# Routing in program order on TensorE, six whole dense columns, and one chain for the last norms

## The chip, the cores and the metric

One core of one Trainium2 chip (trn2). The metric is the device time of one execution of the kernel in microseconds (us), as the median of the runs. Engines: TensorE (PE), VectorE (DVE), ScalarE (ACT), GpSimd (POOL), SyncE (SP), which here only issues DMAs.

## The reference

One decoder layer on 512 tokens of 1024 numbers (four tiles of 128 tokens, 0 to 3): attention and a state-space part first, then an expert stage (PEER), then a last norm. The change touches the expert stage and the last norm:

```python
def peer_ffn(x, w_q, sub1, sub2, u_tab, v_tab):          # x: normed tokens
    q = (xb @ w_q).reshape(b, 128, 8, 256)                # 8 heads
    s1 = einsum('bchd,kd->bchk', q[..., :128], sub1)      # scores against 128 subkeys
    s2 = einsum('bchd,kd->bchk', q[..., 128:], sub2)
    v1, i1 = top_k(s1, 16);  v2, i2 = top_k(s2, 16)
    top, sel = top_k(v1[..., :, None] + v2[..., None, :], 16)   # of 256 sums
    eidx = (i1 * 128 + i2)[sel]                           # 16 of 16384 experts, per head
    gate = softmax(top)
    hid = einsum('bcd,bchkd->bchk', xb, u_tab[eidx])
    act = gelu(hid) * gate
    return einsum('bchk,bchkd->bcd', act, v_tab[eidx])

h = h + peer_ffn(rms_norm(h, ffn_norm), ...)
return rms_norm(h, final_norm)                            # h * rsqrt(mean(h*h) + 1e-6) * g
```

## The kernel before

All instructions of four engines are recorded by a wrapper at line 134 (`Ordered`), so nearly every row of the trace has L134; rows are told apart by their operands. A tile scheduler orders each engine's instructions by its own model of costs, except where `with ordered(...)` is open: there the named engines keep the order in which the code issues them. Each engine then runs its instructions strictly in that order.

The expert stage has two forms. Tiles 0 and 1 are *sparse*: for each of 128 (head, k) pairs an expert step (`peer()`, `Steps`) gathers the u and v rows of that expert for 128 tokens by an indirect DMA from POOL (1.05 MB into one of five slots, `X` and `X4` in the trace), DVE makes the dot of u with the tokens (`CUSTOM_DVE_ANT_0`, its sum read out by a second instruction into `hid`), ACT makes the gelu, and v times the activation is added to h. For tile 0's last 20 steps (k from 108) this last part is done on PE: ACT scales the identity by the activation (`dg`), two fp32 matmuls of 128x512 add into two banks, and `flush()` adds the banks to h on DVE after step 127. The slot of a step is free for a new gather when its matmuls are done. Then `final(0, ...)` norms tile 0 and stores it.

Tiles 2 and 3 are *dense*: every one of 16384 experts is computed for their 256 tokens. For this `route([Topk(2), Topk(3)], ..., 256)` finds the gates of both tiles. It goes through 4 units of 2 heads. A unit has two banks of two times 8 fp32 matmuls 128x256 (q), an ACT copy of each bank, four matmuls with `c_subT` per tile (scores, into one bank per tile), and on DVE four scans of each bank (`first`) and the second top-k (`heads`). When all units are done `finish` transposes a tile's indices and gates on PE with `c_ident` (three 128x128 each) into a table `dtab`. The loop around it (`for w in rest()`) issues tile 0's last expert steps between the pieces of the routing.

Between the routing and the dense loop DVE works on 32 groups of `gate_tokens` (one 128x1024 and three 128x512 f16 products each), which turn `dtab` into the gates of the first 64 columns. The gates of the other 64 are made inside the loop, in its columns up to 61.

`dense()` loops over 128 columns j of 128 experts. Of each, a U half and a V half of 512 KB are loaded by SP (`load`, three buffers `raw`). ACT copies a half to fp32r (`hi`), DVE subtracts that from the raw one (`lo`), which frees the buffer and loads the next. PE then computes hid in 24 fp32r matmuls 128x256 (hi x hi, hi x lo, lo x hi), ACT the gelu (`gS`), DVE the product with the gates, ACT and DVE split that too (`acthi`, `actlo`), and `outp` adds 12 fp32r matmuls 128x512 into four banks. Each column also carries one sparse step of tile 1: a dot, two small ACT steps and an add on DVE. The loop runs with DVE, ACT, PE and POOL in program order. In it, tile 1's `final` is issued in the column of its last step.

After the loop the four banks are added to h of tiles 2 and 3 (held in HBM meanwhile), and `final` is run for each: a square with sum on ACT (`rms`), a chain of small DVE steps for the reciprocal square root (tiles `f_s`, `f_r`, `f_ri`), a scaling by it and the norm's weights, and one store of 512 KB.

Of the kernel before, what the change touches and what calls it, by code (L numbers as in the profile page):

```python
# [12 lines left out]
F32 = mybir.dt.float32  # L13
# [3 lines left out]
I32 = mybir.dt.int32  # L17
U32 = mybir.dt.uint32
AF = mybir.ActivationFunctionType
ALU = mybir.AluOpType  # L20
# [3 lines left out]
D = 1024  # L24
SEQ = 512
NT = 4
EPS = 1e-6
# [4 lines left out]
JC = 64  # L32
DENSE = (2, 3)
# [124 lines left out]
def paced(w, g):  # L158
    for _ in g:
        yield w  # L160
# [3 lines left out]
def hymba_kernel(ctx: ExitStack, tc: tile.TileContext, a, out, dbg=None):  # L164
    nc = tc.nc
    pins = set()
    V, S, G, PE = (Ordered(tc, e, n, pins) for e, n in ((nc.vector, "V"), (nc.scalar, "S"), (nc.gpsimd, "G"), (nc.tensor, "PE")))
    SP = nc.sync

    @contextmanager  # L170
    def ordered(*names):
        pins.update(names)
        yield
        pins.difference_update(names)
# [46 lines left out]
    def ct(name, shape, dt=F32):  # L221
        return cst.tile(list(shape), dt, name=name)


    def rsqrt(dst, src, tmp, itmp):
        V.tensor_scalar(itmp, src.bitcast(I32), -0.5, 1597463007.0, op0=ALU.mult, op1=ALU.add)
        y = itmp.bitcast(F32)
        for _ in range(3):
            V.tensor_tensor(tmp, y, y, op=ALU.mult)
            V.tensor_tensor(tmp, tmp, src, op=ALU.mult)  # L230
            V.tensor_scalar(tmp, tmp, -0.5, 1.5, op0=ALU.mult, op1=ALU.add)
            V.tensor_tensor(dst, tmp, y, op=ALU.mult)
            y = dst

    def rms(src, junk, n="n"):

        s2 = tiny.tile([128, 1], F32, name=n + "_s2")
        r2 = tiny.tile([128, 1], F32, name=n + "_r2")
        r1 = tiny.tile([128, 1], F32, name=n + "_r1")
        ri = tiny.tile([128, 1], I32, name=n + "_ri")  # L240
        S.activation(junk, src, AF.Square, accum_out=s2)
        V.tensor_scalar(s2, s2, 1.0 / D, EPS, op0=ALU.mult, op1=ALU.add)
        rsqrt(r2, s2, r1, ri)
        return r2
# [68 lines left out]
    dtab = msl.v([128, 4, 256], F16, off=4480)  # L313
# [9 lines left out]
    junk = ct("junk", [128, D], BF)  # L323
# [761 lines left out]
    def final(T, h, junk):  # L1085
        r2 = rms(h, junk, "f")
        V.scalar_tensor_tensor(h, h, r2, fn, op0=ALU.mult, op1=ALU.mult)
        SP.dma_start(out[T * 128:(T + 1) * 128, :], h)
# [146 lines left out]
    def dense(xh, xl, sp):  # L1235


        NE, n, done = 128, 128 - sp.k, 0
        acc = [bank() for _ in range(4)]
        his, los = [], []  # L1240
        raws = [lp.tile([128, 2048], F32, name=f"raw{i}") for i in range(2)] + [l01[0].v([128, 2 * D])]
        for i in range(2):
            his.append(lp.tile([128, 2048], F32R, name=f"hi{i}"))
            los.append(lp.tile([128, 2048], F32R, name=f"lo{i}"))
        acts = [lp.tile([128, 2, 256], F32R, name=f"act{i}") for i in range(2)]
        gS = [msl.v([128, 256], off=2048 + 1024 * i) for i in range(2)]
        half = (slice(0, D), slice(D, 2 * D))
        ring = [collections.deque(r[:, o] for r in raws) for o in half]
        loaded, hb = [{}, {}], {}

        def load(n):
            if ring[n] and nload[n] < NE:
                raw, j = ring[n].popleft(), nload[n]
                nload[n] += 1
                SP.dma_start(raw, a["uvt"][j][:, half[n]])  # L1255
                loaded[n][j] = raw

        def hi(j, n):
            if j < NE:
                S.activation(his[j % 2][:, half[n]], loaded[n][j], AF.Copy)  # L1260

        def lo(j, n):
            if j < NE:
                o = half[n]
                V.tensor_tensor(los[j % 2][:, o], loaded[n][j], his[j % 2].bitcast(F32)[:, o], op=ALU.subtract)
                ring[n].append(loaded[n].pop(j))
                load(n)

        def hid(j):
            if j < NE:  # L1270
                uh, ul = his[j % 2], los[j % 2]
                hb[j] = bank()
                for k in range(8):
                    ks = slice(128 * k, 128 * k + 128)
                    for i, (l, r) in enumerate(((uh, xh), (uh, xl), (ul, xh))):
                        PE.matmul(hb[j][:, 0:256], l[:, ks], r[:, k], start=(k == 0 and i == 0), stop=(k == 7 and i == 2))

        def gelu(j):
            if j < NE:
                b = hb.pop(j)  # L1280
                S.activation(gS[j % 2], b[:, 0:256], AF.Gelu_apprx_tanh)
                bfree(b)

        def gated(j):
            if j < NE:
                g = gS[j % 2].rearrange("p (q t) -> p q t", t=32)
                V.tensor_tensor(g, g, gates_of(j), op=ALU.mult)

        def acthi(j):
            if j < NE:  # L1290
                S.activation(acts[j % 2][:, 0], gS[j % 2], AF.Copy)

        def actlo(j):
            if j < NE:
                act = acts[j % 2]
                V.tensor_tensor(act[:, 1], gS[j % 2], act.bitcast(F32)[:, 0], op=ALU.subtract)

        def outp(j):
            (ah, al), vh, vl = (acts[j % 2][:, i] for i in range(2)), his[j % 2][:, D:], los[j % 2][:, D:]
            for t in range(2):  # L1300
                ts = slice(128 * t, 128 * t + 128)
                for i, (l, r) in enumerate(((ah, vh), (ah, vl), (al, vh))):
                    for n in range(2):
                        PE.matmul(acc[2 * t + n], l[:, ts], r[:, 512 * n:512 * n + 512], start=(j == 0 and i == 0),
                                  stop=(j == NE - 1 and i == 2), skip_group_check=True)

        def gate_group(j):

            for g in range(32):
                if 8 * (g // 4) - 1 + 2 * (g % 4) == j:  # L1310
                    return gate_parts(1, 8 * g, junk.bitcast(F32)[:, 0:256])
            return iter(())

        nload = [0, 0]
        for i in range(3):
            load(0)
            load(1)
        ngp = gate_group(-1)
        for i in range(2):
            hi(0, i)  # L1320
            lo(0, i)
        hid(0)
        gelu(0)
        hi(1, 0)
        lo(1, 0)
        for t0 in range(0, 256, 8):
            gate_tokens(0, t0)
        M.small = collections.deque(s for s in M.small if s.parent is nl)
        with ordered("V", "S", "PE", "G"):
            gated(0)  # L1330
            acthi(0)
            actlo(0)
            next(ngp)
            for j in range(NE):
                gp, ngp = ngp, gate_group(j)
                step = sp.k < 128 and (j + 1) * n > done * SPREAD
                hi(j + 2, 0)
                hi(j + 1, 1)
                next(gp, None)
                next(ngp, None)  # L1340
                if step:
                    sp.dot()
                hid(j + 1)
                if step:
                    sp.gelu()
                lo(j + 2, 0)
                gelu(j + 1)
                next(gp, None)
                gated(j + 1)
                next(gp, None)  # L1350
                acthi(j + 1)
                if step:
                    sp.add()
                    done += 1
                actlo(j + 1)
                outp(j)
                lo(j + 1, 1)
                if sp.k == 128 and step:
                    final(sp.T, xs[sp.T], junk)
                if j == 100:  # L1360
                    for i in range(2):
                        SP.dma_start(row(7)[:, half[i]], hsave[i])
        assert sp.k == 128
        for i, T in enumerate(DENSE):
            xs[T] = row(7)[:, half[i]]
            for n in range(2):
                V.tensor_tensor(xs[T][:, 512 * n:512 * n + 512], acc[2 * i + n], xs[T][:, 512 * n:512 * n + 512], op=ALU.add)
            final(T, xs[T], raws[i][:, 0:D])


    proj_k(0, w_k[1], G)
# [24 lines left out]
    for x in SEQN:  # L1396
# [12 lines left out]
        elif x == "F":  # L1409
# [3 lines left out]
            xs = [half(l01[0], 1)]  # L1413
# [12 lines left out]
    g2, fn = half(nl, 0), half(nl, 1)  # L1426
# [51 lines left out]
    W = dict(glu=0.75, k=3.45, c=2, q=3, cmp=3.45, att=0.45, mix=1.725, r1=1, route=0.65, gates=0.4)  # L1478
    NR = 2

    def rest():
# [48 lines left out]
        rl = []  # L1530
# [11 lines left out]
        yield from paced(W["r1"], both(route([Topk(1)], lambda k: X1[k // 4][:, k % 4], 128), later(), NR))  # L1542
        M.free(rl[0], *x1)
        state["p1"] = True
        yield from paced(W["route"], route([Topk(2), Topk(3)], lambda k: rl[1].v([128, 8, 256])[:, k], 256))
        M.free(rl[1])
        G.iota(io2, pattern=[[1, 128], [0, 2]], base=0, channel_multiplier=0, allow_small_or_imprecise_dtypes=True)
        M.group()
# [122 lines left out]
```

## Time and profile before

| | us |
|---|---|
| median of 3 runs | 1604.41 |
| lowest and highest run | 1602.51, 1612.80 |
| the profiled execution | 1603.72 |
| its span in the trace | 1602.0 |
| busy over the span: PE, DVE, ACT, POOL | 1374.4, 1460.7, 838.6, 524.4 |

The order of the stages in the span: attention and the state-space part with the sparse steps of tile 0 beside them up to about 640 us; the routing of tiles 2 and 3 with tile 0's last steps, to 772; gates and the first splits, to 833; the dense loop to about 1587; the last norms. In the rows, a timeline line is: start in us, duration in us, engine, line, operation, out<-in, count, and in brackets the idle time before it with what ended that. A line of the table by stretch is: from:to, length, busy time (and count) of PE, PE's weight loads, DVE, ACT and POOL, then the granted TensorE clock (1.00 is full speed), the share of DMA engines busy and GB/s. Records of fp32 matmuls come in pairs: one matmul is two records.

### The profile page before, as it was taken

The numbers are of one execution on the slowest core, as the hardware profiler recorded it, in microseconds if no ns is written. First come the engines' busy times: TensorE is split into PE (matmuls) and PEld (weight loads), VectorE is DVE, ScalarE is ACT, GpSimd is POOL, SyncE is SP. The second block draws the span as 40 slices with busy tenths as digits, with TensorE's granted clock in tenths as the row PEclk, the third lists the DMA queues.
The fourth block names the chain that finished last, engine by engine and source line by source line (L and its number), as shares of the span: only waits on it lengthen the run. The fifth ranks groups of instructions, "written<-read, shape, count | busy, mean of one in ns | idle before, by whom it ended". The sixth has DMA issues, their size and how long they took to land.

```text
span 1602.0 us, 24306 instructions
## 1 busy us (share of the span) xinstructions
PE 1374.4 (86%) x8400; PEld 1094.4 (68%) x8400; DVE 1460.7 (91%) x3324; ACT 838.6 (52%) x2078; POOL 524.4 (33%) x383
## 2 busy tenths in 40 slices
PE   5688794689868687897679999999999999999996
PEld 2366472456355355772468888888888999999995
DVE  8986179969899989799999999999999999999998
ACT  2345423646366654326565555555555555556563
POOL 6532012744352442012003333333333333333331
PEclk9897897788879799898659999999999999999998
DMA  6331478878898889318508999999999999999994
GB/s 265 106 106 66 172 285 298 337 315 337 325 373 333 315 340 419 131 52 342 211 3 327 334 344 337 343 332 340 341 340 363 388 374 382 374 375 375 378 375 168
DMA packets 88969, 469.48 MB, mean 293 GB/s; under 512 B 10253, under 2 KB 10893, under 8 KB 50701
## 3 DMA queue, kind: packets, MB, share of 16 engines
q0 software_dynamic: 37152, 268.98, 42.9%
q1 hardware_dynamic: 51692, 198.94, 34.4%
q8 instruction: 66, 1.08, 0.3%
q14 instruction: 59, 0.48, 0.1%
HBM read 464.74 MB, written 3.15 MB: 292 GB/s over the span
## 4 chain that ended last, share of the span: by engine, by line
DVE 25%; PE 22%; issue 4%; ACT 1%; DMA 1%; SPq 0%
PE bank L134 22%; DVE X L134 11%; DVE lo L134 8%; DVE junk L134 3%; DVE act L134 2%; DMA raw<-in_uvt 1%; ACT X L134 0%; DVE f_r L134 0%; DVE hid L134 0%; ACT hi L134 0%; ACT junk L134 0%; ACT raw L134 0%; DVE more L134 0%; ACT act L134 0%; SPq L1255 0%
## 5 line engine op out<-in xcount | busy, mean ns | idle before, releaser
L134 POOL DMA_INDIRECT X<-in_uv,eidx x256 | 430.7, 1682 | 955.2 <-DVE X L134 830.5
L134 ACT ACTIVATE X<-bank 128x256 f32<-128x256 f32 (+5 forms) x431 | 218.0, 520 | 181.7 <-PE bank L134 130.6
L134 PE MATMUL bank<-X 128*128 128x64 f16 (+10 forms) x1800 | 243.2, 285 | 71.0 <-DVE X L134 50.0
L134 PE MATMUL bank<-hi,act 128*128 128x512 f32 x1024 | 299.7, 394 | 0.0
L134 PE MATMUL bank<-XH,hi 128*128 128x256 f32 x1024 | 289.4, 283 | 2.5 <-ACT hi L134 2.5
L134 PE MATMUL bank<-XH,lo 128*128 128x256 f32 x1024 | 288.1, 281 | 0.0
L134 PE MATMUL bank<-XL,hi 128*128 128x256 f32 x1024 | 287.9, 281 | 0.0
L134 DVE CUSTOM_DVE_ANT_0 junk<-X 128x1024 bf16<-128x1024 f32 x206 | 250.6, 1217 | 8.0 <-DMA X<-in_uv,eidx 5.4
L134 DVE SCALAR_TENSOR_TENSOR X<-X,act 128x1024 f32<-128x1024 f32 x194 | 247.6, 1276 | 5.2 <-ACT act L134 5.0
L134 ACT ACTIVATE gt<-hid 128x1 f32<-128x1 f32 x384 | 63.9, 198 | 357.1 <-DVE hid L134 356.9
L134 DVE TENSOR_TENSOR X<-X 128x256 f32<-128x256 f32 (+13 forms) x597 | 229.2, 418 | 22.5 <-ACT X L134 20.0
L134 PE MATMUL bank<-X,X 128*128 128x128 f32 (+5 forms) x1172 | 209.9, 352 | 21.3 <-ACT X L134 11.8
L134 DVE TENSOR_TENSOR lo<-raw,hi 128x1024 fp32r<-128x1024 f32 x172 | 209.4, 1217 | 1.3 <-ACT hi L134 1.3
L134 PEld LDWEIGHTS bank<-hi,act 128*128 128x128 f32 x1024 | 183.3, 188 | 32.7
L134 PEld LDWEIGHTS bank<-XH,hi 128*128 128x128 f32 x1024 | 194.3, 190 | 7.5 <-ACT hi L134 2.6
L134 PEld LDWEIGHTS bank<-XL,hi 128*128 128x128 f32 x1024 | 193.9, 189 | 4.9
L134 PEld LDWEIGHTS bank<-X,X 128*128 128x128 f32 (+3 forms) x1172 | 150.3, 195 | 67.4 <-issue 28.4
L134 PEld LDWEIGHTS bank<-XH,lo 128*128 128x128 f32 x1024 | 194.7, 190 | 0.0
L134 ACT ACTIVATE hi<-raw 128x1024 fp32r<-128x1024 f32 x172 | 178.9, 1052 | 28.6 <-PE bank L134 21.8
L134 PEld LDWEIGHTS bank<-X 128*128 128x128 f32 (+3 forms) x776 | 123.7, 197 | 67.9 <-issue 29.6
L134 PE MATMUL bank<-lo,act 128*128 128x512 f32 x512 | 159.5, 393 | 0.4 <-DVE lo L134 0.4
L134 PEld LDWEIGHTS bank<-lo,act 128*128 128x128 f32 x512 | 95.9, 188 | 22.7 <-DVE lo L134 0.8
(195 smaller groups left out, 1664.0 us busy)
## 6 DMA issues: line engine op xcount, KB each, us to landing
raw<-in_uvt SPq DMA_DIRECT2D x172, 512.0 KB, 6.4
X<-in_uvt SPq DMA_DIRECT2D x84, 512.0 KB, 7.6
X<-in_wq SPq DMA_DIRECT2D x24, 1024.0 KB, 7.8
X<-in_wo SPq DMA_DIRECT2D x8, 1024.0 KB, 16.6
X<-in_x SPq DMA_DIRECT2D x8, 512.0 KB, 4.0
X<-in_wB SPq DMA_DIRECT2D x4, 1024.0 KB, 15.4
X<-in_wA SPq DMA_DIRECT2D x4, 1024.0 KB, 7.6
X<-in_w SPq DMA_DIRECT2D x4, 1024.0 KB, 5.8
```

The costliest lines, as they stand in the source:

```text
L134: ins = self.last = f(*args, **kw)
```

## The change

It has three parts. First, PE keeps the order of the code while tiles 2 and 3 are routed (`with ordered("PE")`). Second, six columns (`whole(j)`: j = 4, 14, 24, 34, 44, 54) don't split their V half or their activations: `outp` takes `gS` and the raw V half in four fp32 matmuls, and the raw buffer is given back there (`done_with`). Third, tile 1's `final` leaves the loop; the sums of squares of three tiles go into one 128x3 tile, one chain computes three reciprocal roots, and six half-width scalings are each followed by a store of 256 KB.

```diff
@@ -1255,16 +1255,23 @@
                 SP.dma_start(raw, a["uvt"][j][:, half[n]])
                 loaded[n][j] = raw
 
+        def whole(j):
+
+            return j < JC and j % 10 == 4
+
         def hi(j, n):
-            if j < NE:
+            if j < NE and not (n and whole(j)):
                 S.activation(his[j % 2][:, half[n]], loaded[n][j], AF.Copy)
 
+        def done_with(j, n):
+            ring[n].append(loaded[n].pop(j))
+            load(n)
+
         def lo(j, n):
-            if j < NE:
+            if j < NE and not (n and whole(j)):
                 o = half[n]
                 V.tensor_tensor(los[j % 2][:, o], loaded[n][j], his[j % 2].bitcast(F32)[:, o], op=ALU.subtract)
-                ring[n].append(loaded[n].pop(j))
-                load(n)
+                done_with(j, n)
 
         def hid(j):
             if j < NE:
@@ -1287,15 +1294,22 @@
                 V.tensor_tensor(g, g, gates_of(j), op=ALU.mult)
 
         def acthi(j):
-            if j < NE:
+            if j < NE and not whole(j):
                 S.activation(acts[j % 2][:, 0], gS[j % 2], AF.Copy)
 
         def actlo(j):
-            if j < NE:
+            if j < NE and not whole(j):
                 act = acts[j % 2]
                 V.tensor_tensor(act[:, 1], gS[j % 2], act.bitcast(F32)[:, 0], op=ALU.subtract)
 
         def outp(j):
+            if whole(j):
+                for t in range(2):
+                    for n in range(2):
+                        PE.matmul(acc[2 * t + n], gS[j % 2][:, 128 * t:128 * t + 128], loaded[1][j][:, 512 * n:512 * n + 512],
+                                  start=False, stop=False, skip_group_check=True)
+                done_with(j, 1)
+                return
             (ah, al), vh, vl = (acts[j % 2][:, i] for i in range(2)), his[j % 2][:, D:], los[j % 2][:, D:]
             for t in range(2):
                 ts = slice(128 * t, 128 * t + 128)
@@ -1355,17 +1369,25 @@
                 actlo(j + 1)
                 outp(j)
                 lo(j + 1, 1)
-                if sp.k == 128 and step:
-                    final(sp.T, xs[sp.T], junk)
                 if j == 100:
                     for i in range(2):
                         SP.dma_start(row(7)[:, half[i]], hsave[i])
         assert sp.k == 128
+        s2, r1, r2, ri = (dtab.bitcast(F32)[:, 0, 4 * i:4 * i + 3] for i in range(4))
+        ri = ri.bitcast(I32)
+        S.activation(junk, xs[sp.T], AF.Square, accum_out=s2[:, 2:3])
         for i, T in enumerate(DENSE):
             xs[T] = row(7)[:, half[i]]
             for n in range(2):
                 V.tensor_tensor(xs[T][:, 512 * n:512 * n + 512], acc[2 * i + n], xs[T][:, 512 * n:512 * n + 512], op=ALU.add)
-            final(T, xs[T], raws[i][:, 0:D])
+            S.activation(raws[i][:, 0:D], xs[T], AF.Square, accum_out=s2[:, i:i + 1])
+        V.tensor_scalar(s2, s2, 1.0 / D, EPS, op0=ALU.mult, op1=ALU.add)
+        rsqrt(r2, s2, r1, ri)
+        for n in range(2):
+            for i, T in ((2, sp.T), (0, DENSE[0]), (1, DENSE[1])):
+                o = slice(512 * n, 512 * n + 512)
+                V.scalar_tensor_tensor(xs[T][:, o], xs[T][:, o], r2[:, i:i + 1], fn[:, o], op0=ALU.mult, op1=ALU.mult)
+                SP.dma_start(out[T * 128:(T + 1) * 128, o], xs[T][:, o])
 
 
     proj_k(0, w_k[1], G)
@@ -1542,7 +1564,8 @@
         yield from paced(W["r1"], both(route([Topk(1)], lambda k: X1[k // 4][:, k % 4], 128), later(), NR))
         M.free(rl[0], *x1)
         state["p1"] = True
-        yield from paced(W["route"], route([Topk(2), Topk(3)], lambda k: rl[1].v([128, 8, 256])[:, k], 256))
+        with ordered("PE"):
+            yield from paced(W["route"], route([Topk(2), Topk(3)], lambda k: rl[1].v([128, 8, 256])[:, k], 256))
         M.free(rl[1])
         G.iota(io2, pattern=[[1, 128], [0, 2]], base=0, channel_multiplier=0, allow_small_or_imprecise_dtypes=True)
         M.group()
```

How the order on the engines changes, at three places. The bank, slot and `dg` names in the rows are those of the program; a number behind x counts equal rows in sequence.

On PE, at the start of the routing's first unit, after the last two transposes of the tokens, before:

```order
L134 MATMUL bank0_83<-X_76 128x256 x4
L134 MATMUL bank7_90<-X_76 128x256 x4
L134 MATMUL bank6_89<-X_76 128x256 x3
L134 MATMUL bank0_83<-X_76 128x256 x12
L134 MATMUL bank7_90<-X_76 128x256 x12
L134 MATMUL bank4_87<-c_subT_132,X4_77 128x128 x2
L134 MATMUL bank5_88<-c_subT_132,X4_77 128x128 x2
L134 MATMUL bank2_85<-X_76 128x256 x9
L134 MATMUL bank4_87<-c_subT_132,X4_77 128x128 x2
L134 MATMUL bank5_88<-c_subT_132,X4_77 128x128 x2
```

and now:

```order
L134 MATMUL bank0_83<-X_76 128x256 x16
L134 MATMUL bank7_90<-X_76 128x256 x16
L134 MATMUL bank4_87<-c_subT_132,X4_77 128x128 x4
L134 MATMUL bank5_88<-c_subT_132,X4_77 128x128 x4
L134 MATMUL bank2_85<-X_76 128x256 x16
L134 MATMUL bank6_89<-X_76 128x256 x16
```

The four scores of a tile (bank4_87 for tile 2, bank5_88 for tile 3) stood behind 35 and 44 matmuls of q (banks 83, 90, 89, 85); now all stand behind 32.

On PE, at the end of the routing, before; dg_5104 is the matrix of the first of tile 0's last 15 expert steps:

```order
L134 MATMUL bank7_90<-X_76,dg_5083 128x512
L134 MATMUL bank0_83<-X4_77,dg_5104 128x512
L134 MATMUL bank7_90<-X4_77,dg_5104 128x512
L134 MATMUL bank0_83<-X4_77,dg_5125 128x512
L134 MATMUL bank7_90<-X4_77,dg_5125 128x512
L134 MATMUL bank0_83<-X_76,dg_5129 128x512
L134 MATMUL bank7_90<-X_76,dg_5129 128x512
L134 MATMUL bank0_83<-X_76,dg_5133 128x512
L134 MATMUL bank7_90<-X_76,dg_5133 128x512
L134 MATMUL bank0_83<-X_76,dg_5146 128x512
L134 MATMUL bank7_90<-X_76,dg_5146 128x512
L134 MATMUL bank3_86<-c_subT_132,X4_77 128x128 x2
```

and now:

```order
L134 MATMUL bank7_90<-X_76,dg_5083 128x512
L134 MATMUL bank4_87<-c_ident_105,X5_78 128x128 x3
L134 MATMUL bank0_83<-X4_77,dg_5104 128x512
L134 MATMUL bank7_90<-X4_77,dg_5104 128x512
L134 MATMUL bank0_83<-X4_77,dg_5125 128x512
L134 MATMUL bank7_90<-X4_77,dg_5125 128x512
L134 MATMUL bank0_83<-X_76,dg_5129 128x512
L134 MATMUL bank7_90<-X_76,dg_5129 128x512
L134 MATMUL bank5_88<-c_ident_105,X5_78 128x128 x3
L134 MATMUL bank0_83<-X_76,dg_5133 128x512
L134 MATMUL bank7_90<-X_76,dg_5133 128x512
```

Five expert steps stood ahead of the last unit's scores (bank3_86); now all scores stand ahead of them, and tile 2's closing transposes (c_ident into bank4_87) too.

On DVE, around tile 0's last dots (ISA rows with `junk` are the dots, those with `hid` alone the reading of the sum), before:

```order
L134 ISA junk_138,hid_5207<-X_76 128x1024
L134 ISA hid_5207 128x1
L134 MAX_INDEX X4_77<-X5_78,bank3_86 128x8
L134 MATCH_REPLACE X5_78<-X5_78,bank3_86 128x128
L134 MAX_INDEX X5_78<-X5_78,X4_77 128x8
L134 MAX X5_78<-X4_77 128x8
L134 MAX_INDEX X5_78<-X5_78,bank1_84 128x8
```

and now:

```order
L134 ISA junk_138,hid_5249<-X_76 128x1024
L134 ISA hid_5249 128x1
L134 ISA junk_138,hid_5263<-X_76 128x1024
L134 ISA hid_5263 128x1
L134 ISA junk_138,hid_5277<-X_76 128x1024
L134 ISA hid_5277 128x1
L134 TENSOR_TENSOR X_76<-bank0_83,X_76 128x512
L134 TENSOR_TENSOR X_76<-bank7_90,X_76 128x512
```

Before, a dot stood in every ten or so rows of the top-k's scans; now the last ten dots stand behind the whole of it and three gate groups, with few or no rows between them, and the two adds of the flush close them.

## Rows read from the trace of the kernel before

**Rows 1.** Busy time by stretch: end of the routing, gates, first half of loop.

```profile
712.00:772.00 60.00, 41.53 (x99) 16.77 (x97) 59.83 (x297) 33.10 (x128) 19.64 (x18) 0.91 0.79 302
722.00:728.00 6.00, 4.01 (x5) 1.80 (x6) 6.00 (x31) 4.98 (x19) 0.00 (x0) 0.51 1.01 425
772.00:832.87 60.87, 41.37 (x536) 34.01 (x537) 57.99 (x146) 36.99 (x36) 0.00 (x0) 0.53 0.27 101
832.87:1222.00 389.13, 378.20 (x2756) 340.85 (x2754) 385.16 (x564) 220.12 (x407) 125.72 (x62) 0.99 0.91 331
```

**Rows 2.** Timeline of DVE: first scans of score banks, with DVE's wait.

```profile
669.36 0.30 DVE L134 MAX8 X<-bank 128x8 f32<-128x128 f32 x1 [10.12 <-PE bank L134]
...
711.85 0.30 DVE L134 MAX8 X<-bank 128x8 f32<-128x128 f32 x1 [1.16 <-PE bank L134]
```

**Rows 3.** Timeline of PE: the routing's first q matmuls.

```profile
648.06 16.04 PE L134 MATMUL bank<-X 128*128 128x256 f32 x70
```

**Rows 4.** Timeline of PE: tile 0's expert steps and the closing transposes.

```profile
723.99 5.64 PE L134 MATMUL bank<-X,dg 128*128 128x512 f32 x8 [5.73 <-ACT dg L134]
...
770.51 1.01 PE L134 MATMUL bank<-c_ident,X 128*128 128x128 f32 x6 [2.48 <-DVE X L134]
```

**Rows 5.** Timeline of POOL: issue of two gathers.

```profile
216.10 1.09 POOL L134 DMA_INDIRECT X<-in_uv,eidx  x1 [49.55 <-issue]
...
728.05 0.94 POOL L134 DMA_INDIRECT X<-in_uv,eidx  x1 [8.57 <-PE bank L134]
```

**Rows 6.** Timeline of DVE: dots, flush, and products of the gates.

```profile
222.36 1.22 DVE L134 CUSTOM_DVE_ANT_0 junk<-X 128x1024 bf16<-128x1024 f32 x1 [0.29 <-DMA X<-in_uv,eidx]
...
719.93 1.20 DVE L134 CUSTOM_DVE_ANT_0 junk<-X,X 128x1024 bf16<-128x1024 f32 x1
...
763.13 1.20 DVE L134 CUSTOM_DVE_ANT_0 junk<-X 128x1024 bf16<-128x1024 f32 x1
...
767.59 0.68 DVE L134 TENSOR_TENSOR X<-bank,X 128x512 f32<-128x512 f32 x1
...
771.60 1.29 DVE L134 TENSOR_TENSOR X<-X 128x1024 f16<-128x1024 f16 x2
...
773.08 0.75 DVE L134 TENSOR_TENSOR X<-X 128x512 f16<-128x512 f16 x2
```

**Rows 7.** Timeline of DVE in one dense column.

```profile
1002.60 0.42 DVE L134 TENSOR_TENSOR act<-X,act 128x256 fp32r<-128x256 f32 x1
1002.93 1.22 DVE L134 TENSOR_TENSOR lo<-raw,hi 128x1024 fp32r<-128x1024 f32 x1
1004.07 0.68 DVE L134 TENSOR_TENSOR X<-X 128x1024 f16<-128x1024 f16 x1
```

**Rows 8.** Timeline of PE: an output product's span, and fp32 matmuls of its shape.

```profile
610.22 3.60 PE L134 MATMUL bank<-X,more 128*128 128x512 f32 x8
613.65 3.60 PE L134 MATMUL bank<-X,X 128*128 128x512 f32 x8
...
843.85 0.63 PE L134 MATMUL bank<-hi,act 128*128 128x512 f32 x2
...
846.60 0.28 PE L134 MATMUL bank<-XH,hi 128*128 128x256 f32 x1
```

**Rows 9.** DMA issues of the dense loads, and ACT in a dense column.

```profile
raw<-in_uvt SPq DMA_DIRECT2D x172, 512.0 KB, 6.4
...
1012.46 0.20 ACT L134 ACTIVATE gt<-hid 128x1 f32<-128x1 f32 x1 [2.74 <-DVE hid L134]
```

**Rows 10.** Timeline of the tail, DVE and ACT.

```profile
1588.90 0.15 DVE L134 TENSOR_SCALAR f_s<-f_s 128x1 f32<-128x1 f32 x1
1589.09 0.15 DVE L134 TENSOR_SCALAR f_ri<-f_s 128x1 int32<-128x1 int32 x1
...
1591.35 1.06 ACT L134 ACTIVATE raw<-X 128x1024 f32<-128x1024 f32 x1 [1.44 <-DVE f_r L134]
...
1596.82 1.28 DVE L134 SCALAR_TENSOR_TENSOR X<-X,f_r 128x1024 f32<-128x1024 f32 x1
```

## The prediction, made before the result was known

> **What bounds the kernel now.** I read four views, in this order: busy time by stretch, the VectorE (DVE) timeline, the GpSimd (POOL) timeline with its row gathers, and the TensorE (PE) timeline. In the table by stretch [rows 1] DVE is busy 59.83 of 60.00 us in the last part of the routing, 57.99 of 60.87 us between the routing and the dense loop, and 385.16 of 389.13 us in the first half of the loop. PE is busy 41.53, 41.37 and 378.20 us there. So DVE ends last in all three places that the change touches, and an edit is worth what it takes from DVE or adds to DVE's waits. Inside the loop PE is close behind: 10.9 us idle in 389.
>
> The profiled execution took 1603.7 us (span 1602.0, 1.7 outside), 0.7 under the median of 1604.4. The sum goes against 1603.7.
>
> **Part 1: program order on PE in the routing.** It takes no instruction away. It moves PE's work for tiles 2 and 3, and with it the last 15 expert steps of tile 0.
>
> What it gives. DVE idles 10.12 us before its first scan of a score bank and 1.16 us at a later one [rows 2]. PE begins the q matmuls at 648.06 and does the first 35 in 16.04 us, 0.46 us each (a 128x256 fp32 matmul is two records) [rows 3]. Before, 44 of them and half of the scores stand ahead of the first complete score bank; now 32 do. Twelve fewer is 5.5 us; in program order PE has to wait for ScalarE's copy of the last q bank, for which I take 0.4 off: 5.1 us. The later waits (1.16 and a smaller one, 1.4 in all) go as well, since the scores no longer stand behind expert steps.
>
> What it costs. An expert step of tile 0 is: POOL gathers one 1.05 MB set of rows into one of five slots, DVE makes a dot, ScalarE a diagonal matrix, PE two fp32 matmuls; these free the slot for the gather five steps on. Before, the matmuls of step 1 run at 723.99 as soon as their matrix is there [rows 4], and gather 6 is issued at 728.05, after 8.57 us in which POOL waited for PE [rows 5]. So the loop of gather, dot and matmul is hidden: DVE always has scans of the top-k to do between dots. Now the closing transposes of tile 2, which need the end of tile 2's top-k on DVE, stand ahead of those matmuls on PE, and no step on PE gets past them. DVE's order is fixed too: five dots, the rest of the top-k, three gate groups, then ten dots back to back, then the two adds (the flush) that read PE's sums. The ten dots no longer have scans between them.
>
> Worked out, from rows of before:
> - The transposes run at 770.51 [rows 4]. Ahead of them go 5.1 + 1.4 us of waits, ten dots of 1.135 us (a dot's 1.20 us with the overlap of its end, 11.4) and one flush add with its overlap (1.2) that now come later [rows 6]: 751.5.
> - Transposes 1.0 us [rows 4], then step 1's matmuls, 723.99 to 728.05 = 4.06 us [rows 4, 5]. The granted clock around them is 0.51, the lower of TensorE's two levels (1.2 GHz); I take the same, since PE again comes from a wait. Gather 6 goes at 756.6.
> - From a gather's start to its dot with nothing else in the way: 216.10 to 222.36, 6.3 us [rows 5, 6]. Dot 6 at 762.9.
> - The other nine gathers follow at the rate that memory gives: 1.05 MB at the 425 GB/s of 722 to 728 us [rows 1] is 2.5 us. Last dot at 762.9 + 22.5 = 785.4.
> - From the last dot's start to the flush 4.46 us (763.13 to 767.59) [rows 6]: 789.9, so 22.3 us later than 767.59.
> - DVE does in that time what it did after the flush before: the top-k's last work 1.5, four casts and differences of the transposes, some 0.2 each, 0.8, three gate groups (one 128x1024 at 0.65 and three 128x512 at about 0.35, 1.65 each) 4.8 [rows 6]: 7.1 us. The 1.3 us in which DVE then waited for ScalarE to convert the first column should vanish, as DVE arrives later.
>
> The loop begins 22.3 - 7.1 - 1.3 = 14 us later. The same by idle time: 21 us of new waits between dots, less 5.1 and 2.8, is 13.
>
> Bounds: 8 us, if step 1 runs at the 1.6 us of the second step in the row at 723.99 (5.64 - 4.06) and a gather lands about 2 us sooner, with the top-k ending 2 us earlier; 19 us, if gathers pace at the 3.1 us at which the dots of before were spaced (719.93 for dot 1, 763.13 for dot 15, 14 gaps [rows 6]). I take 14, nearest to rows of the same transfer.
>
> The Trainium skill ("DMA: Bandwidth & Descriptors", section "Anatomy of one DMA — SWDGE (gpsimd) path") puts such a transfer at 2.0 us and its bytes at 436 GB/s, an estimate of 4.4 us for 1.05 MB. The trace shows 6.3 from start to dot, and by the page the loss would be 12 us.
>
> **Part 2: six whole columns.** In each, DVE drops the V half's difference (1002.93, next start 1004.07: 1.14 us) and the small one of the activations (0.33) [rows 7]: 1.47 us, 8.8 for six. PE swaps twelve fp32r matmuls, 843.85 to 846.60 or 2.75 us, for four in fp32; eight records of that shape took 3.43 us [rows 8]: 0.68 more, 4.1 for six. PE's 10.9 us of idle in [rows 1] holds that in the half where five of the six columns stand (all six are at j up to 54 of 128). ScalarE drops two copies and is not the bound.
>
> The raw V half is now given back by the output matmuls, about a column later, and its next load goes behind that on SP's queue. A load takes 6.4 us to land [rows 9], and about 5 are left before its first reader: 1.4 us late. ScalarE's wait of 2.74 us in the column [rows 9] covers it. Without that cover it would be six times 1.4, or 8 us, which would eat the gain. I take -8.5, some 0.3 lost to the moments in which DVE waits for the gelu; bounds -8.8 and +4.1 (PE's extra in full, nothing from DVE).
>
> The Trainium skill ("FP8 and Floating Point Precision", section "TensorE Precision Notes") counts four passes for true fp32. That speaks against the edit: sixteen passes in place of twelve, an estimate of 0.9 us a column. The row gives 0.68.
>
> **Part 3: the last norms.** The tail has three chains of small DVE steps about 0.19 us apart; the third square starts at 1591.35, 1.44 us late, as it waits for a piece of the second chain, and the last scaling starts at 1596.82 and takes 1.28 [rows 10]. One chain of 14 steps (2.7 us) after the third square, then six half-width scalings of about 0.6, end some 1.6 us earlier, and the last store is half as large. Six stores for three on an idle queue add no end of their own. I take -1.7; bounds -3 and 0 (if all is held by the landing of the last store).
>
> **Sum:** 1603.7 + 14.0 - 8.5 - 1.7 = 1607.5 us.
>
> **Rivals.**
> - The waits are covered (a gain of part 1 alone). If ScalarE and PE let the slots go as early as before, or DVE has other work ready between the dots, only 5.1 + 1.4 us of part 1 stay: 1603.7 - 6.5 - 8.5 - 1.7 = 1587. For it: the scores' waits are real rows. Against it: DVE runs in a fixed order, and that order has the ten dots side by side.
> - PE binds in the loop, so whole columns give nothing. PE has 97% busy there, and its 4.1 us more would show in full: 1607.5 + 8.5 + 4.1 = 1620. For it: the small margin, above all if the later V loads also hit. Against it: 10.9 us idle on PE, under 4 on DVE.
> - Slower: PE stays at the lower level through the expert steps after the transposes. A step then takes 4.06 us in place of 1.6, more than the 2.5 us of a gather, and PE's ten remaining steps set the pace of the slots: steps 1 to 5 end at 756.6 to 772.9, step 10 at 793, dot 15 at 799, flush at 805, 15 us on: 1622.5. It decides from the point at which a step is longer than 2.5 us. For it: the granted clock of 0.53 from 772 to 833 us [rows 1]. Against it: the second step of the row at 723.99 already takes 1.6 us, and the five queued steps leave PE without a gap.
>
> **How the numbers follow.** A run of this kernel can tell about 1% from no change: 1588.4 and 1620.4. I give the forecast 0.66, the covered waits 0.10, the PE bound 0.12 and the low clock 0.12. The forecast's own range, with part 1 from +8 to +19, part 2 from -8.8 to -4 and part 3 from -3 to 0, is 1600 to 1619. The range for all cases is 1592 to 1622: it leaves out the covered waits and a little of the low clock. Faster by over 1%: most of the covered waits and a trace of the forecast, 0.07. Slower: two thirds of the low clock, half of the PE bound (1620 lies at the line) and 0.02 of the forecast, 0.16. The rest, 0.77, lies within 1%.
>
> **What would show it.** Right: the first scan near 664; transposes of tile 2 near 751 and PE's expert steps behind them; POOL waiting some 35 us for PE before gather 6; DVE waiting 1 to 6 us at most of the last ten dots; the loop's start near 847. In the loop a whole column has no V difference, DVE still without gaps and a shorter stretch by 1.4 us. One f_r chain at the end. Wrong: gather 6 before 740, no idle time at the dots, or PE waiting for nothing in the loop while DVE waits for gelu.

## The result and the profile after

| | us |
|---|---|
| before, median of 7 runs | 1604.41 |
| after, median of 7 runs (lowest, highest) | 1622.24 (1615.00, 1624.01) |
| ratio after to before, 95% interval | 1.0086 [1.0062, 1.0109], or 13.8 us more |
| predicted | 1607.5 (3.8 us more than the 1603.7 from which the sum starts), range 1592 to 1622 |
| profiled execution of after, its span | 1623.39, 1621.4 |

The change makes the kernel slower by 0.9%. The ratio compares the means of the seven runs (1606.6 and 1620.5 us), and by it the changed kernel stands at 1618, in the upper part of the range and within the 1% that the forecast gave 0.77. The margin is small: the upper end of the interval is 1.0109, and the median itself, 1622.24, lies 0.2 us above the range. The loss of part 1 was larger than the sum had it.

The two profiles can't be compared by absolute times. The first q matmul of the routing starts at 648.06 before and at 654.64 after, though the change moves nothing ahead of it. In the ten other profiles of this study that start lies between 645.0 and 660.4, whatever the kernel. So all times below are counted from that matmul (t = 0) where they are compared.

| us from the first q matmul | before | after | predicted for after |
|---|---|---|---|
| first complete score bank scanned | 21.3 | 17.4 | 16.2 |
| tile 2's closing transposes | 122.5 | 104.5 | 103.4 |
| gather 6 issued | 80.0 | 109.1 | 108.5 |
| dot 6 | 86.3 | 114.7 | 114.8 |
| last dot of tile 0 | 115.1 | 140.5 | 137.3 |
| flush | 119.5 | 144.6 | 141.8 |
| first gated product of the loop | 186.2 | 207.8 | 200 |

TensorE's timeline of the changed kernel (columns as in the rows of before):

```profile
654.64 15.93 PE L134 MATMUL bank<-X 128*128 128x256 f32 x64
...
732.97 8.75 PE L134 MATMUL bank<-X,dg 128*128 128x512 f32 x20
759.18 0.90 PE L134 MATMUL bank<-c_ident,X 128*128 128x128 f32 x3 [17.46 <-DVE X L134]
759.87 7.49 PE L134 MATMUL bank<-X,dg 128*128 128x512 f32 x12
...
798.02 1.98 PE L134 MATMUL bank<-X,dg 128*128 128x512 f32 x4 [1.00 <-ACT dg L134]
```

This is the mechanism of the prediction in one view, against [rows 4]. PE stands still for 17.46 us in front of the transposes, which wait for DVE. The dots of steps 1 to 5 ran from 741.47 to 753.42, but their matmuls stand behind the transposes in the order; PE may not take them sooner. GpSimd's timeline shows who waits for that:

```profile
741.99 1.49 POOL L134 DMA_INDIRECT X<-in_uv,eidx  x1 [0.77 <-PE bank L134]
763.77 1.24 POOL L134 DMA_INDIRECT X<-in_uv,eidx  x1 [20.28 <-PE bank L134]
765.91 0.95 POOL L134 DMA_INDIRECT X<-in_uv,eidx  x1 [0.91 <-PE bank L134]
```

Between gather 5 and gather 6 POOL waits 20.28 us for PE; in [rows 5] it waited 8.57. The prediction had expected some 35: it had not seen that the first five gathers come later too (gather 5 at 87.4 us from the first q matmul, 70.5 before). And DVE's timeline shows what that does to the dots, which were without idle time before [rows 6]:

```profile
672.01 0.30 DVE L134 MAX8 X<-bank 128x8 f32<-128x128 f32 x1 [6.18 <-PE bank L134]
...
769.36 1.23 DVE L134 CUSTOM_DVE_ANT_0 junk<-X,X 128x1024 bf16<-128x1024 f32 x1 [0.55 <-DMA X<-in_uv,eidx]
...
786.88 1.23 DVE L134 CUSTOM_DVE_ANT_0 junk<-X,X 128x1024 bf16<-128x1024 f32 x1 [2.65 <-DMA X<-in_uv,eidx]
...
799.19 0.69 DVE L134 TENSOR_TENSOR X<-bank,X 128x512 f32<-128x512 f32 x1 [2.86 <-PE bank L134]
...
809.77 1.23 DVE L134 TENSOR_TENSOR lo<-raw,hi 128x1024 fp32r<-128x1024 f32 x1 [3.48 <-ACT hi L134]
```

The sum of DVE's waits over the whole stretch from the first scores to the loop's first columns says the same in one row per cause (waited for: us in total, times, longest). Before, 655 to 875 us:

```profile
DVE X L134 <- PE bank L134: 12.1, 4, 10.1
DVE X L134 <- ACT X L134: 2.2, 1, 2.2
DVE lo L134 <- ACT hi L134: 1.3, 2, 0.8
DVE act L134 <- ACT act L134: 0.5, 1, 0.5
```

After, the same stretch:

```profile
DVE X L134 <- PE bank L134: 12.6, 9, 6.2
DVE X L134 <- ACT X L134: 6.2, 2, 4.0
DVE junk L134 <- DMA X<-in_uv,eidx: 5.9, 4, 2.6
DVE junk L134 <- ACT act L134: 5.1, 4, 1.3
DVE lo L134 <- ACT hi L134: 3.5, 1, 3.5
DVE junk L134 <- ACT dg L134: 1.7, 1, 1.7
DVE act L134 <- ACT act L134: 0.5, 1, 0.5
DVE X L134 <- issue: 0.5, 1, 0.5
```

16.1 us have become 36.0. The 10.1 at the first scores fell to 6.2; of the rest only the wait of 0.5 for `act` is as it was, all others are new or longer.

The stretch from the flush to the loop, before (columns as in [rows 1]):

```profile
767.59:834.21 66.62, 44.16 (x550) 35.98 (x549) 62.26 (x164) 40.11 (x43) 1.39 (x1) 0.56 0.30 111
```

and after:

```profile
799.19:862.45 63.26, 40.70 (x528) 33.27 (x527) 55.22 (x136) 38.01 (x38) 0.94 (x1) 0.57 0.32 117
```

DVE's work there fell by 7.0 us, as predicted (7.1). Its idle time did not fall by 1.3 but rose from 4.4 to 8.0. The largest part of that is a wait for ScalarE's conversion of the first column, whose load has a new condition. What SP waited for just ahead of that load, before (issued at 770.74) and after (at 800.13), is

```profile
SPq L1255 <- DVE X L134: 5.9, 1, 5.9
...
SPq L1255 <- PE bank L134: 3.3, 1, 3.3
```

In the loop, from the split of the first column's activations to that of the last, 747.5 us became 740.5. The first 65 columns before and after:

```profile
834.21:1235.21 401.00, 389.88 (x2841) 351.24 (x2840) 398.33 (x581) 226.80 (x422) 129.76 (x64) 1.00 0.91 333
```

```profile
862.45:1256.48 394.03, 388.10 (x2817) 343.56 (x2817) 390.08 (x570) 220.52 (x410) 125.06 (x64) 1.00 0.93 340
```

DVE works 8.25 us less, the stretch is 6.97 shorter, and the rest of the loop is the same to 0.01 us. In ACT's and DVE's timelines stands one place behind the last whole column, j = 54:

```profile
1206.86 1.06 ACT L134 ACTIVATE hi<-raw 128x1024 fp32r<-128x1024 f32 x1 [4.31 <-DMA raw<-in_uvt]
...
1208.64 0.42 DVE L134 TENSOR_TENSOR X<-X 128x256 f32<-128x256 f32 x1 [1.29 <-ACT X L134]
```

There a half that was loaded late outlasts ScalarE's 2.74 us of cover [rows 9], and DVE waits 1.29 us. Of the six whole columns it is the only one behind which DVE waits.

The tail, against [rows 10], on DVE and SP:

```profile
1611.36 0.37 DVE L134 TENSOR_SCALAR X<-X 128x3 f32<-128x3 f32 x2 [1.21 <-ACT raw L134]
...
1614.15 4.06 DVE L134 SCALAR_TENSOR_TENSOR X<-X 128x512 f32<-128x512 f32 x6
1614.93 3.64 SPq L1390 DMA_DIRECT2D out_dram<-X  x6
```

One chain of 2.8 us, six scalings of 0.68 us; from the last split to the end of the span 17.5 us in place of 19.4.

So by these two traces part 1 costs 21.7 us (207.8 - 186.2), part 2 brings 7.0 and part 3 brings 1.9: 12.8 us in all, beside the 13.8 of the runs. Four further profiles below have the routing without program order; their first gated product stands at 186.4 to 187.5, so the cost of part 1 is 20.4 to 21.7 us, depending on the profile that it is read against.

### The profile page after: what moved, and what is told of

Its sections match the earlier page's. It is cut to its first block, busy times and chain, and to the rows that moved or that the text cites. A ratio compares the mean times of both kernels' runs of the same rounds, so it can differ in the third digit from the quotient of the medians.

```text
span 1621.4 us, 24206 instructions
## 1 busy us (share of the span) xinstructions
PE 1377.9 (85%) x8376; PEld 1091.4 (67%) x8376; DVE 1452.0 (90%) x3287; ACT 834.3 (51%) x2066; POOL 520.2 (32%) x383
## 4 chain that ended last, share of the span: by engine, by line
DVE 40%; PE 35%; issue 13%; DMA 6%; ACT 3%; POOL 2%; SPq 0%; DVEq 0%; POOLq 0%; ACTq 0%
PE bank L134 35%; DVE X L134 24%; DVE lo L134 7%; DVE junk L134 5%; DMA X<-in_uv,eidx 4%; ACT X L134 2%; POOL X L134 2%; DVE act L134 1%; DMA raw<-in_uvt 1%; DVE nm L134 0%; DMA X<-in_wq 0%; DMA X<-in_x 0%; ACT gt L134 0%; DVE zT L134 0%; DVE more L134 0%
## 5 line engine op out<-in xcount | busy, mean ns | idle before, releaser
L134 POOL DMA_INDIRECT X<-in_uv,eidx x256 | 425.6, 1662 | 977.8 <-DVE X L134 828.3
L134 PE MATMUL bank<-hi,act 128*128 128x512 f32 x976 | 285.2, 394 | 0.0
L134 DVE TENSOR_TENSOR X<-X 128x256 f32<-128x256 f32 (+15 forms) x606 | 231.5, 415 | 26.3 <-ACT X L134 21.0
L134 PE MATMUL bank<-X,X 128*128 128x128 f32 (+5 forms) x1172 | 214.2, 357 | 24.5 <-ACT X L134 13.7
L134 DVE TENSOR_TENSOR lo<-raw,hi 128x1024 fp32r<-128x1024 f32 x168 | 204.6, 1218 | 3.6 <-ACT hi L134 3.5
L134 PEld LDWEIGHTS bank<-hi,act 128*128 128x128 f32 x976 | 174.8, 188 | 30.9
L134 ACT ACTIVATE hi<-raw 128x1024 fp32r<-128x1024 f32 x168 | 175.5, 1053 | 36.1 <-PE bank L134 23.0
L134 PE MATMUL bank<-lo,act 128*128 128x512 f32 x488 | 151.9, 392 | 0.4 <-DVE lo L134 0.4
L134 PEld LDWEIGHTS bank<-lo,act 128*128 128x128 f32 x488 | 91.5, 188 | 21.6 <-DVE lo L134 0.8
## 6 DMA issues: line engine op xcount, KB each, us to landing
X<-in_wB SPq DMA_DIRECT2D x4, 1024.0 KB, 16.2
```

The lines of the kernel that those rows point to most:

```text
L134: ins = self.last = f(*args, **kw)
```

## The experiments

All are compared with runs of the kernel before, taken beside them on the same chip; the ratio has its 95% interval behind it. "Without part 1" below means the first of these runs; the other profiles with its order of the routing give 186.2 to 186.6 where it gives 187.5.

**Without part 1.** The `with ordered("PE")` of the routing is taken out of the changed kernel.

```diff
-        with ordered("PE"):
-            yield from paced(W["route"], route([Topk(2), Topk(3)], ...
+        yield from paced(W["route"], route([Topk(2), Topk(3)], ...
```

> The changed kernel without part 1 (no program order on TensorE in the routing); whole columns and the one chain stay. Theory (part 1 alone loses the time, about 21.7 us in the traces): loop 7.0 shorter and tail 1.9 shorter than before, so 0.9945 of before, about 1595 us, and the dense loop starts where it did before (DVE's first gated product near 834). Rival (the whole columns or the new tail also disturb what comes before them, or the early 6.6 us belong to the change): above 0.999.

Measured: 0.9937 [0.9917, 0.9957]; loop 740.9, tail 17.6, first gated product 187.5 us from the first q matmul. Parts 2 and 3 are worth what the traces gave them (0.9945 was expected), and part 1 alone turns the gain into a loss. The rival falls; this profile also starts its routing late (at 660.4), without part 1.

**Part 1 alone**, on the kernel before.

> The kernel before with part 1 alone. Theory: the loop starts 21.7 us later relative to the first q matmuls, nothing else moves: ratio 1.0135, about 1626 us. Rival (the loss is the 14 us of the prediction and the rest was chance in one profile): 1.0087, about 1618.

Measured: 1.0126 [1.0090, 1.0161]; loop 747.6, first gated product 207.7. The interval just leaves out 1.0087, from four runs, and holds 1.0135: the loss is some 20 us, not the 14 of the prediction. The trace says the same (207.7 - 186.2 = 21.5).

**Program order up to the last scores**, the closing transposes outside it:

```diff
+        r23 = route([Topk(2), Topk(3)], ...
+        with ordered("PE"):
+            for _ in range(60):
+                next(r23)
+                yield W["route"]
+        yield from paced(W["route"], r23)
```

> The changed kernel with program order on TensorE only until the last scores; the closing transposes of both tiles are issued outside it, so TensorE may take six of tile 0's expert steps before them. Theory (the transposes in front of the expert steps hold the slots): gather 6 goes some 4 to 10 us after gather 5, not 20; the dots still come late, since all steps stand behind the last unit's scores, so some waits at the dots stay: loop start about 13 to 16 us sooner than in the changed kernel, ratio about 0.999 (0.996 to 1.003). Rival (the loss comes from the order of q and scores, or from dots that are late as such): within 4 us of the changed kernel, 1.006 or more.

Measured: 0.9999 [0.9982, 1.0015]. In GpSimd's timeline gather 6 now stands 7.5 us behind gather 5:

```profile
739.18 1.49 POOL L134 DMA_INDIRECT X<-in_uv,eidx  x1 [0.77 <-PE bank L134]
746.73 0.94 POOL L134 DMA_INDIRECT X<-in_uv,eidx  x1 [6.06 <-DVE X L134]
```

POOL's 20 us of waiting for PE are gone and with them 12.5 us of the loop's start (195.4 for 207.8). So the transposes ahead of the steps are 12.5 us of the loss, a little under the 13 to 16 that were expected. The other 8 (195.4 against the 187.5 without part 1) are still there: the dots begin at 87.4 us, where they began at 73.2 without part 1. All steps stand behind the fourth unit's scores here; what that costs is seen in the next run.

**Program order for three of four units** (`range(45)` in the same place).

> As the run before, but program order on TensorE only for the first three of the four units; the last unit's scores and all of tile 0's last 15 steps are free, and DVE's order has the dots among scans again, about one in ten rows. Theory: the earlier first scores (3.9 us) stay, little of the loss does: ratio 0.992 to 0.996, so at or below the kernel without part 1. Rival (program order of the first units costs by itself, for example by a TensorE that waits for ScalarE's copies of q): 0.998 or more.

Measured: 0.9951 [0.9928, 0.9974]. With the fourth unit free the loop starts at 189.5, 5.8 us sooner than in the run before. The first scores come at 17.6, but the loop still starts 2.1 later than without part 1: the step that its theory wanted, at or below that kernel, was missed. The dots begin at 77.1, and DVE waits 3.4 us for ScalarE's first conversion. So the three units in order take back more than the 5 us that they give at the first scores.

**Program order for two of four units** (`range(30)`).

> The changed kernel with program order on TensorE for the first two of the four units only. In the order the first unit's scores then stand behind 32 matmuls of q, as in the changed kernel, and VectorE's rows have the dots as spread as before. Theory: the first scores come 4 to 5 us sooner as in the changed kernel, and the expert steps lose nothing: loop start 3 to 4 us sooner than without part 1, ratio 0.990 to 0.993. Rival (what comes sooner at the first unit is waited for again at the next ones, or the first steps come later with the second unit's scores ahead of them): 0.994 to 0.996, no better than without part 1.

Measured: 0.9911 [0.9884, 0.9938]; first scores at 20.1, first dot at 70.2, first gated product at 183.3, which is 4.2 sooner than without part 1 and 2.9 to 3.3 sooner than in the other four profiles with that order. In DVE's timeline the first wait is

```profile
673.58 0.30 DVE L134 MAX8 X<-bank 128x8 f32<-128x128 f32 x1 [8.94 <-PE bank L134]
```

The expected 4 to 5 us at the first scores are missed. In this trace only four records of scores stand behind the first 64 of q; the other twelve stand behind 20 records more. The first scores are 2.5 us sooner than without part 1 (22.6), but half of that is TensorE's clock, as the last section shows; against the kernel before (21.3), whose clock rose as early, it is 1.2. DVE waits only 0.6 us at a dot and not at all for the conversion of the first column. So by the traces a part of the gain of part 1 can be had without its loss. The runs don't show it by themselves: the interval overlaps with that of the run without part 1.

**Program order for the last unit and the transposes alone** (45 pieces free, then `with ordered("PE")`).

> The changed kernel with program order on TensorE for the last of the four units and the closing transposes only. Theory (the whole loss lies in the last unit and the transposes, the gain in the first unit): the loss of the changed kernel without its gain, so the loop starts some 22 to 27 us later than without part 1, ratio 1.007 to 1.011. Rival (a part of the loss comes from the order of the first three units): 1.004 or less.

Measured: 1.0135 [1.0092, 1.0178]; first scores at 22.7, gather 6 with 20.99 us of waiting for PE ahead of it, first gated product at 214.4, 26.9 later than without part 1 (22 to 27 expected; the ratio is above the expected 1.007 to 1.011, with an interval that reaches into it). The last unit and the transposes alone cost more than the changed kernel loses, which has the gain at the first scores beside it. But that doesn't clear the first three units: three of them in order cost time by themselves, as shown above, and the two costs taken alone (26.9 and 2.1 us) don't add up to the changed kernel's loss. Freed one after the other from the changed kernel, the transposes give 12.5 us, the fourth unit 5.8 and the first three 2.1.

**Part 3 alone.**

> The kernel before with part 3 alone (one chain and six half-width stores; no program order on TensorE in the routing, no whole columns). Theory: from the last split of the activations to the end of the span 17.5 us in place of 19.4, the loop 747.5 as before: ratio 0.9988. Rival (the loop also gains, since tile 1's last norm leaves it): loop 746 or less, 0.998 or less.

Measured: 0.9973 [0.9954, 0.9991]; loop 747.6, tail 17.5. The trace gives the 1.9 us and no more; the ratio's interval holds 0.9988.

**Thirteen whole columns** (`j % 5 == 4`), without part 1.

> Parts 2 and 3 with thirteen whole columns (every fifth of the first 64) in place of six. Theory (TensorE becomes the bound: in the loop of the kernel before it is idle 0.36 us in a pair of columns, 0.9 in five, and a whole column costs it 0.68): a whole column then gains only 0.22 us, the loop takes 744.6 us, longer than the 740.9 with six columns; ratio to the kernel before 0.996. Rival (VectorE is the bound throughout and each whole column gives what the six gave, 1.17 us): loop 732 us, ratio 0.989.

Measured: 0.9904 [0.9867, 0.9942]; loop 736.4, so 11.1 us less than before. Both expectations fall, one on each side: 0.85 us a column. The idle time that I read off the busy column was too small. In the kernel before nearly every gate group's 16 small matmuls take 0.78 us up to the next matmul; where PE is the bound (the run with twenty-one columns) the same groups take 0.49 to 0.50. The records count the whole 0.78 as busy. What PE needs is read where it is the bound: a column without gate group takes 5.58 us (345.85 us for 62 columns), a gate group 0.5, a whole column 0.68 more. For 65 columns with 32 gate groups that is 378.6 + 0.68 n us on PE, against 401.0 - 1.47 n on DVE: they meet at n = 10.4 (10.9 with the 1.38 us a column that DVE's busy time fell by in the changed kernel). The row of thirteen columns stands 2.5 us over PE's line (387.4):

```profile
834.22:1224.14 389.92, 388.78 (x2793) 338.12 (x2793) 382.18 (x558) 214.76 (x398) 137.62 (x64) 1.00 0.93 343
```

Late loads may add to it: ScalarE waits 24.3 us for raw halves in eleven places, in the kernel before nowhere. How much of that reaches the loop's time was not separated.

**Twenty-one whole columns** (`j % 3 == 1`), to test that line.

> Parts 2 and 3 with 21 whole columns (every third of the first 64). Theory (TensorE binds beyond some ten columns): the first 65 columns take at least 378.6 + 21 x 0.68 = 392.9 us, so longer than the 389.9 with thirteen; ratio above that with thirteen, 0.992 or more. Rival (VectorE is still the bound): about 381 us, ratio 0.985.

Measured: 0.9941 [0.9919, 0.9963]. PE is busy without a gap, and the stretch is 393.41 us, 0.5 from the line:

```profile
836.79:1230.20 393.41, 393.41 (x2755) 330.61 (x2754) 370.54 (x539) 208.50 (x380) 113.59 (x64) 1.00 0.91 339
```

**Two units in order and ten whole columns**, put together:

```diff
-            return j < JC and j % 10 == 4
+            return j < JC and j % 6 == 4
```

> The candidate that should beat both kernels: program order on TensorE for the first two units only, ten whole columns (every sixth of the first 64), the one chain for the norms. Theory, with TensorE's real slack (a column without a gate group takes 5.58 us where TensorE is the bound, a gate group 0.5, a whole column 0.68 more; 65 columns are then 378.6 + 0.68 n on TensorE, and 401.0 - 1.47 n on VectorE, which meet at n = 10.4): loop about 735 us, start as with program order on two units: ratio 0.987 to 0.989. Rival (late loads of the V half take it back): loop 739 or more, ratio 0.991 or more.

Measured: 0.9900 [0.9878, 0.9923], loop 734.7, first gated product 184.1: 16 us under the kernel before and, by the two ratios, 30 under the changed one. The ratio misses the expected 0.987 to 0.989 by a little. The loop is the shortest of all runs, about where it was expected (735); its first 65 columns take 388.2 us, 1.9 over the 386.3 of DVE's line. The first scores come only at 21.3, with TensorE's clock rising late (last section). The runs don't tell this kernel from the one with thirteen columns and no program order (0.9904).

## Why the prediction was right, and where it was short

The direction, the place and the mechanism held. Gather 6, dot 6 and the transposes came within 1.1 us of the working, in part because small errors cancel: the transposes were 1.1 us late, dot 6 0.1 early. The three rivals fell: the waits are not covered (the loop starts 21.7 us later), PE does not bind with six columns (the loop gained 7.0), and the low clock did not last: the granted clock is 0.71 from 759 to 768 us, where the first three steps behind the transposes take 2.5 us each, and 1.00 from 768 to 800, where a step runs at 1.98, not at 4.06. The sum failed in its first term: part 1 was put at 14 us, with 19 as its upper bound, and is 21.7 (20.4 at the least). The time came out within 1% although that term was off by more than half of its size; with an interval from 1.0062 to 1.0109 that took some luck. The pieces, each against the step that priced it:

- "The 1.3 us in which DVE then waited for ScalarE [...] should vanish, as DVE arrives later." This step is wrong and the largest piece, 5.0 us with the waits around it: the wait of 1.3 us became 3.5, and short waits for PE behind the flush grew by 1.4. SP issues the first column's loads when the last expert step is over (800.13, against 798.02 + 1.98 for its matmuls), so they move with the flush and DVE does not arrive later than they do. Before, they were issued 2.7 us after the last step. What had covered the load was work behind the flush, and 7 us of it had gone ahead.
- The last ten dots at 2.5 us: six gaps of 2.5 to 2.8, but three of 3.0 to 3.9; 25.7 us in place of 22.5. With 0.5 less in the pieces around it that is 2.7 us at the flush. These two pieces are the 7.7 us between 14 and 21.7.
- The gain at the first scores, 5.1 us: 3.9 against the profile before. The 32 matmuls took 15.93 us, 0.50 each, where the row of before had 0.46. Between profiles in which TensorE's clock rose late in both (22.6 without part 1, 17.4 with it) it is 5.2, so the price was right and the row of before was a fast one. This piece is made up for ahead of dot 6.
- DVE's work ahead of the flush, 7.1 us: 7.0. The working has a slip (three gate groups of 1.65 us are 5.0, not 4.8), which changes nothing.

The second term, -8.5, measured -7.0. The 1.47 us a column was near (DVE's busy time fell by 8.25, 1.38 a column, and two units in order with six columns have a first stretch of 392.66, 8.3 less than before). What failed is "ScalarE's wait of 2.74 us in the column [rows 9] covers it": it does so in five columns of six, and the sixth cost 1.3 us. The third term, -1.7, measured -1.9.

In the profile without part 1 four fp32 matmuls take 3.5 us in a whole column (875.55 to 879.18 for the second matmul behind them, less its 0.12) where the twelve took 2.75: 0.75 more. That lies between the 0.68 of the row and the estimate of 0.9 that the prediction worked out from the passes in the Trainium skill ("FP8 and Floating Point Precision", "TensorE Precision Notes"). Gather 6 took 5.6 us from issue (763.77) to its dot (769.36). That lies between the 6.3 of the row and the estimate of 4.4 from the Trainium skill ("DMA: Bandwidth & Descriptors", "Anatomy of one DMA — SWDGE (gpsimd) path").

Not settled: why DVE's busy time falls by 1.38 us a column and not by 1.47, and how the loss would change if the first raw load were issued ahead of the last expert step. Neither was tried.

## What to carry to other kernels

- An engine kept in program order is blocked by whatever stands at its head. Before pinning one, look for instructions that wait on another engine's last result (here transposes) and ask which ring of buffers is freed by the instructions behind them; pin only the stretch where the order pays.
- When a transfer is moved and the work that covered it is moved ahead of it, count the wait at its far end anew; a wait does not vanish because the waiting engine is late too.
- Trading work between two engines has an optimum where their lines meet. Read an engine's real need where it is the bound, not from its busy time where it waits inside a group.

## What the runs showed of the hardware

Six kernels have the same order of q at the start of the routing. Their first 70 records of q take 16.04 us before and 15.95 with part 3 alone, but 17.38 to 17.50 in the other four (without part 1, thirteen columns, twenty-one columns, the last unit in order). Over the 23.7 us from the first q matmul the granted clock is 0.97 in the first two and 0.91 in the other four. TensorE had waited 14.5 us for DVE ahead of the transposes in front of these matmuls, in all of them.

```profile
649.76 15.95 PE L134 MATMUL bank<-X 128*128 128x256 f32 x70
...
660.36 17.38 PE L134 MATMUL bank<-X 128*128 128x256 f32 x70
```

The six kernels that begin with program order show the same two groups: 64 records take 14.87 us with two units in order, and 15.93 to 16.30 in the other five, the changed kernel among them. So the time until TensorE returns to 2.4 GHz after the same wait differs from one profile to the next by some 1.1 to 1.5 us of work. That is as much as the gain at the first scores was short of its price, and it has to be taken off where first scores of two profiles are compared.
